# Another order of loads at the start of stick-breaking attention, and other places for two sets of transposes

## The chip, the cores and the metric

The kernel runs on one core of a Trainium2 chip. The metric is the device time of one execution in microseconds (us), the median of several runs. The core has TensorE (matmuls and transposes; PE in the profile, PEld its weight loads), VectorE (DVE), ScalarE (ACT), GpSimd (POOL) and SyncE (SP). In this kernel SP issues most loads and POOL most stores; each works through its queue in order, so an issue that waits holds up all that stand behind it.

## The reference

One step of an encoder layer for a prompt of 1024 tokens and a sample of 32 tokens with a cache of 512, model width 1024, everything in float32. What matters here:

```python
ada = silu(c) @ w_ada + b_ada        # (1024 x 6144): shift1, scale1, gate1, shift2, scale2, gate2
h   = rms_norm(x, g_pre_mix) * (1 + scale1) + shift1
p   = h @ w_in                       # q-latent | kv-latent | rope key | q_b | k_b | v_b | gate A | gate B
z   = einsum('bqhd,bshd->bhqs', q_b, k_b) * 64 ** -0.5      # stick-breaking attention, 8 heads of 64
sp  = where(mask, softplus(z), 0);  later = cumsum(sp, reverse) - sp
o_b = einsum('bhqs,bshd->bqhd', where(mask, exp(log_sigmoid(z) - later), 0), v_b)
```

The new rows of k_b and v_b are outputs too. Latent attention (o_a), two gated projections, an output projection and a gated convolutional feed-forward layer follow; conv_w, conv_b, g_pre_ffn and the latent gains are vectors that these later stages need.

## The kernel before, in words

**Products.** Each float32 operand is held as a high part (rounded to fp32r) and a low part (the rest), and a product takes three fp32r matmuls: high by high, high by low, low by high. Splitting costs one ScalarE instruction for the high part (`hi`, L65) and one VectorE subtraction for the low one (`lo`, L68). A weight tile of 128 columns is loaded by SP into a `wr` buffer of 128 x 1024 (two buffers) and split into `wh` and `wl` (two buffers each); a `wr` buffer is free once its split is done.

**Stages.** `stage_h` makes h, transposed. `stage_qkv` makes the queries, keys and values of the stick-breaking heads. `stage_sb` runs that attention, with the gate columns of w_in and the adaptive weights as fill. `stage_lat`, `stage_mla`, `stage_merge`, `stage_up` and `stage_down` follow.

**`stage_qkv`.** The column tiles are 128 wide; tile p holds heads 2p and 2p + 1. First the query tile 0, the key tile 0 (copied to S0, whose first 1024 columns are also called S1) and one latent tile (`lf`) are made one by one, in three blocks of 352 tokens by `mtile`. The other ten tiles are made in five pairs by `pair`: each pair is computed as seven half-size products on sums and differences of the two weights (`ra`, `rb`) and of h (T1 to T4, made by `sums`). The sums of weights are written to S1 (L575, L576). Each finished tile is handed to `after`: a key tile gets a high part (`KH`, in an `sg` buffer, of which there are two), nine transposes into natural row order that are copied (L462) and stored to the output (L468) in three steps, and at the end its low part, in place; `spill` (L449) stores high and low parts in DRAM scratch (`qh`, `ql`, `kh`, `kl`). Value tiles go to `vd`. The steps of `after` are a generator, put in the list `back`; `bg(n)` advances it by n steps. For the key tile 0 this is `bg(4)`, behind all three blocks of the latent tile and behind the store of it (`l2d`, L645).

**Late vectors.** `late_vectors` (called behind the second pair) loads nine rows of vectors into an `sg` buffer by POOL, transposes them in seven transposes (L159) and copies them out.

**The start of `stage_sb`.** The pools of `stage_qkv` are released and the new ones take their place. On the right side lie, in order of address, T4, T3, T1, T2 (two tiles of 8448 bytes a partition each), ending at h; the new pool `sb` (V1, KL1, Q1, KH1, small tiles, V0, KL0, Q0, KH0, 4096 bytes each) ends at the same edge, so KL0, Q0 and KH0 lie where T2 lay. A new tile waits only for the old tiles under it. `begin(h)` issues six loads for head h of a pair by `queries` (L1074) and one for V (L1096 in the first pair, L1070 afterwards).

**The order.** In `sb_attend` TensorE, ScalarE and VectorE follow the written list ORDER (manual_schedule); `S0.0` is a score block, `T0.0` a block of transposes, `V3.0` a product with values, `f` one step of the fill, the first digit the head and query block (0 to 3 is the first head, 4 to 7 the second), and `then` hangs loads on entries. S1.1 is the fourth score block and takes the `s` bank of S0.0. The fill is the generator of `gates`: for each of 16 gate tiles two adaptive weights (`ada_step`, L204, 512 KB each, matmuls L206), then 24 steps of three matmuls. Everything else, the queues of SP and POOL and the other engines outside such a section, is ordered by the compiler's scheduler, by readiness and the order of the program. `issue_after(x)` makes what is traced inside it come behind x in the queue of x's engine, without waiting for x to finish. `sb_sample`, traced behind the four pairs, begins with a memset of QZ (L953), a tile of the pool `att`, which takes the place of the released left-side pools.

## Time and profile before

| what | us |
|---|---|
| median of three runs | 1723.23 (1721.87 to 1725.38) |
| the profiled execution | 1717.57 |
| its span, first to last instruction | 1715.8 |
| TensorE busy | 1662.9 |
| VectorE busy | 1272.7 |
| ScalarE busy | 992.6 |
| GpSimd busy | 293.7 |

Times in the profile's rows count from the start of the span. A timeline row gives start, duration, engine, line, operation, tiles (out<-in), shapes, how often, and in brackets the idle time of the engine just before and what ended it. `SPq` and DMA rows are issues, not transfers; a row of DMA issues gives the size of each and the median time from issue to landing. A row of a window gives the stretch and its length, busy time and number of instructions of PE, PEld, DVE, ACT and POOL, the granted clock of TensorE, the share of the DMA engines and GB/s. A row of waits gives the total, how often, and the longest.

### The profile page before, as it was taken

The page shows a single profiled execution, that of the slowest core. Times are in us where ns is not written, and L with a number is a line of the kernel's source. Part 1 is how long each engine was busy: PE and PEld are TensorE (multiplying, and loading weights), DVE is VectorE, ACT ScalarE, POOL GpSimd, SP SyncE. Part 2 cuts the span into 40 slices and gives each one's busy share as a digit, 9 for nine tenths or more (in the row PEclk, how much of TensorE's full clock was granted, in tenths as well). Part 3 has the DMA queues.
Part 4 walks back from the last instruction along what each step waited for, and adds up shares of the span by engine and source line. Part 5 has one row for each costly group of instructions (what it writes and reads, how often), then busy time and mean ns, then how long its engine had stood idle before and what let it go on. Part 6 is the DMA issues. An engine that isn't in the chain of part 4 may idle for free. (4 is left out here: it accounts for less than half of the span.)

```text
span 1715.8 us, 30290 instructions
## 1 busy us (share of the span) xinstructions
PE 1662.9 (97%) x11646; PEld 1514.0 (88%) x11646; DVE 1272.7 (74%) x2129; ACT 992.6 (58%) x1934; POOL 293.7 (17%) x564
## 2 busy tenths in 40 slices
PE   6999799999999999999999999999999999999997
PEld 3999799999899899998889789999999999977885
DVE  4854497979794588888776779887787787788456
ACT  4534386979794567777773376544444444544442
POOL 2113311111111131111000121121121122110013
PEclk8999999999999999999999999999999999999999
DMA  9235687555633331222174531423323333697643
GB/s 328 89 116 185 234 229 199 157 166 164 170 117 94 118 94 53 68 61 73 55 276 149 184 123 50 155 93 129 130 99 133 133 101 134 225 346 243 219 138 120
DMA packets 185984, 255.20 MB, mean 149 GB/s; under 512 B 14702, under 2 KB 125568, under 8 KB 185840
## 3 DMA queue, kind: packets, MB, share of 16 engines
q1 hardware_dynamic: 165712, 194.63, 36.3%
q0 software_dynamic: 19904, 58.56, 9.6%
q8 instruction: 91, 1.49, 0.4%
q14 instruction: 53, 0.43, 0.1%
q10 hardware_dynamic: 224, 0.09, 0.0%
HBM read 187.86 MB, written 64.57 MB: 147 GB/s over the span
## 5 line engine op out<-in xcount | busy, mean ns | idle before, releaser
L65 ACT ACTIVATE wh<-wr 128x1024 fp32r<-128x1024 f32 (+5 forms) x163 | 132.2, 820 | 220.3 <-PE s L2010 81.7
L68 DVE TENSOR_TENSOR wl<-wr,wh 128x1024 fp32r<-128x1024 f32 (+5 forms) x163 | 150.0, 929 | 86.4 <-ACT wh L65 86.0
L72 PE MATMUL mm<-hh,wh 128*128 128x352 f32 x456 | 154.0, 338 | 0.0
L73 PE MATMUL mm<-hl,wh 128*128 128x352 f32 x456 | 149.2, 327 | 0.4 <-DVE hl L302 0.3
L74 PE MATMUL mm<-hh,wl 128*128 128x352 f32 x456 | 148.4, 326 | 0.0
L2009 PE MATMUL mm<-T,wh 128*128 128x256 f32 (+1 forms) x376 | 108.5, 289 | 0.0
L2011 PE MATMUL mm<-T,wl 128*128 128x256 f32 (+1 forms) x376 | 107.5, 287 | 0.3 <-DVE wl L68 0.2
L2010 PE MATMUL mm<-T,wh 128*128 128x256 f32 (+1 forms) x376 | 107.3, 286 | 0.0
L2009 PE MATMUL s<-T,wh 128*128 128x256 f32 (+1 forms) x348 | 99.7, 287 | 2.5 <-ACT wh L65 2.5
L2011 PE MATMUL s<-T,wl 128*128 128x256 f32 (+1 forms) x348 | 99.7, 286 | 0.4 <-DVE wl L68 0.4
L2010 PE MATMUL s<-T,wh 128*128 128x256 f32 (+1 forms) x348 | 99.4, 286 | 0.0
L68 DVE TENSOR_TENSOR wl<-S,wh 128x1024 fp32r<-128x1024 f32 (+1 forms) x55 | 59.3, 1079 | 51.0 <-ACT wh L65 50.7
L72 PEld LDWEIGHTS mm<-hh,wh 128*128 128x128 f32 x456 | 86.4, 189 | 7.3 <-ACT o L756 3.3
L73 PEld LDWEIGHTS mm<-hl,wh 128*128 128x128 f32 x456 | 86.4, 190 | 3.2 <-DVE hl L302 1.8
L2150 DVE SCALAR_TENSOR_TENSOR u<-u,c,u 128x1058 f32<-128x1058 f32 x68 | 87.0, 1317 | 2.1 <-ACT u L2147 0.8
L74 PEld LDWEIGHTS mm<-hh,wl 128*128 128x128 f32 x456 | 86.4, 189 | 0.4 <-issue 0.3
L770 PE MATMUL tr<-c,A 128*128 128x128 f32 x576 | 83.8, 274 | 0.8 <-ACT A L729 0.3
L65 ACT ACTIVATE wh<-S 128x1024 fp32r<-128x1024 f32 (+1 forms) x55 | 51.8, 943 | 46.5 <-PE s L2010 13.4
L2009 PE MATMUL tr<-T,wh 128*128 128x272 f32 (+1 forms) x272 | 77.8, 286 | 0.0
L2011 PE MATMUL tr<-T,wl 128*128 128x272 f32 (+1 forms) x272 | 77.7, 286 | 0.0
L2010 PE MATMUL tr<-T,wh 128*128 128x272 f32 (+1 forms) x272 | 77.4, 284 | 0.0
L770 PEld LDWEIGHTS tr<-c,A 128*128 128x128 f32 x576 | 67.3, 141 | 7.7 <-DVE PTl L68 1.4
(754 smaller groups left out, 5793.7 us busy)
## 6 DMA issues: line engine op xcount, KB each, us to landing
wr<-in_w_ada_dram SPq DMA_DIRECT2D x48, 512.0 KB, 6.4
wr<-in_w_up_dram SPq DMA_DIRECT2D x44, 512.0 KB, 3.9
dr<-in_w_down_dram SPq DMA_DIRECT2D x43, 512.0 KB, 6.0
wr<-in_w_in_dram SPq DMA_DIRECT2D x33, 512.0 KB, 4.7
wr<-gdn SPq DMA_DIRECT2D x30, 512.0 KB, 4.3
gdn<-u POOLq DMA_DIRECT2D x23, 512.0 KB, 5.4
gd<-nat POOLq DMA_DIRECT2D x48, 176.0 KB, 3.7
t<-gd SPq DMA_DIRECT2D x16, 528.0 KB, 5.0
```

The lines of the kernel that those rows point to most:

```text
L65: self.nc.scalar.activation(out, in_, AF.Identity, scale=scale)
L68: return self.nc.vector.tensor_tensor(out, full, hi.bitcast(F32), ALU.subtract)
L72: m(ps, lh, rh, start=start, stop=False)
L73: m(ps, lh, rl, start=False, stop=False)
L74: self.pe = m(ps, ll, rh, start=False, stop=stop).ins
L770: self.nc.tensor.transpose(tr[:, (2 * s + q) * P : (2 * s + q + 1) * P], at[q][:, b * P : b * P + P], self.idt)
L2009: m(ps[:, :n], w[0][:, k], x[0][:, k, c], start=first and k == 0, stop=False, skip_group_check=True)
L2010: m(ps[:, :n], w[0][:, k], x[1][:, k, c], start=False, stop=False, skip_group_check=True)
L2011: i = m(ps[:, :n], w[1][:, k], x[0][:, k, c], start=False, stop=k == 3, skip_group_check=True)
L2150: nc.vector.scalar_tensor_tensor(y, u[:, w : w + YW], self.cvT[:, w, cc : cc + 1], y, ALU.mult, ALU.add)
```

## The change

The first key tile's steps are advanced by two behind each block of the latent tile, in place of four behind the last. The late vectors are loaded behind the second pair and transposed behind the third. All adaptive weights of `ada_step` are queued behind the last of the six query and key loads of the first head of the first pair. The second head's loads are issued in every pair at S2.0a (queries and keys) and S2.1a (values); before, this was so for the first pair alone, both at S2.0a, and for the others at S7.1b and V7.0 of the pair before.

```diff
--- before.py
+++ after.py
@@ -159,15 +159,24 @@
         self.nc.tensor.transpose(ps[:, :n], v, self.idt[:n, :n])
         return ps[:, :n]
 
+    def late_loads(self, v):
+
+        a = self.a
+        rows = [(r0, n, 0, a[g][0]) for r0, n, g in ((0, 8, "g_pre_ffn"), (8, 3, "g_q_lat"), (11, 2, "g_kv_lat"))]
+        rows += [(0, 44, w + 1, a["conv_w"][0, w] if w < 3 else a["conv_b"][0] if w == 3 else a["state_ffn_conv"][0, 0, w - 4])
+                 for w in range(6)]
+        for r0, n, w, x in rows:
+            self.nc.gpsimd.dma_start(v[r0 : r0 + n, P * w : P * w + P], x.rearrange("(k p) -> k p", p=P))
+        return v
+
     def late_vectors(self, v):
 
         nc, a = self.nc, self.a
         ps = self.bank("tr")
         dma = nc.gpsimd.dma_start
-        self.rows_T(ps, v[:13, 0:P], ((0, 8, a["g_pre_ffn"][0]), (8, 3, a["g_q_lat"][0]), (11, 2, a["g_kv_lat"][0])), dma)
+        self.rows_T(ps, v[:13, 0:P], (), dma)
         for w in range(6):
-            x = a["conv_w"][0, w] if w < 3 else a["conv_b"][0] if w == 3 else a["state_ffn_conv"][0, 0, w - 4]
-            self.rows_T(ps[:, 44 * (w + 1) :], v[:44, P * (w + 1) : P * (w + 2)], ((0, 44, x),), dma)
+            self.rows_T(ps[:, 44 * (w + 1) :], v[:44, P * (w + 1) : P * (w + 2)], (), dma)
         nc.vector.tensor_copy(self.gvT[:, 8:21], ps[:, :13])
         nc.vector.tensor_copy(self.cvT.rearrange("p w c -> p (w c)"), ps[:, 44 : 44 * 7])
 
@@ -201,7 +210,8 @@
         ps = self.bank("mm")
         for i, (v, k) in enumerate(self.ada_todo[:n]):
             w = self.tl(pool, [P, D], F32, "wr")
-            nc.sync.dma_start(w, a["w_ada"][0, k * P : (k + 1) * P, v * D : (v + 1) * D])
+            with self.tc.issue_after(self.begun):
+                nc.sync.dma_start(w, a["w_ada"][0, k * P : (k + 1) * P, v * D : (v + 1) * D])
             for j in range(4):
                 nc.tensor.matmul(ps[32 * j : 32 * j + 32, :256], self.cT[:, k], w[:, j * 256 : j * 256 + 256],
                                  start=i == 0, stop=i == n - 1)
@@ -642,12 +652,14 @@
         raws = [(raw(col("v", 0)), raw(col("v", 1)))]
         for c0, n, ps in self.mtile(wh, wl, self.Hh, self.Hl, self.BLK, KT, "mm mm pv"):
             nc.scalar.copy(lf[:, c0 : c0 + n], ps[:, :n])
+            bg(2)
         nc.gpsimd.dma_start(self.l2d, lf)
-        bg(4)
         for i, (ta, tb) in enumerate(pairs):
             pair(i, ta, tb, *U[i % 2 * 2 : i % 2 * 2 + 2])
             if i == 1:
-                self.late_vectors(sg().bitcast(F32))
+                late = self.late_loads(sg().bitcast(F32))
+            elif i == 2:
+                self.late_vectors(late)
         self.in_w.append(self.w_in_tile(2208))
         for r, c in self.SB:
             nc.gpsimd.dma_start(self.sbd[r, c], self.sb[r, c])
@@ -1066,7 +1078,8 @@
         t = lambda n: self.tl(S, [P, TP], F32R, n)
 
         def values(p, h):
-            V[h] = t(f"V{h}")
+            if p:
+                V[h] = t(f"V{h}")
             nc.sync.dma_start(V[h].bitcast(F32).rearrange("r (t d) -> r t d", t=8), self.vd[p][:, :, h])
 
         def queries(p, h):
@@ -1079,7 +1092,7 @@
             d(KH[h][o], "kh")
             d(Q[h][o], "ql")
             d(self.KLz[h][r], "kl")
-            d(self.KLz[h][o], "kl")
+            return d(self.KLz[h][o], "kl").ins
 
         def first(h):
             V[h], self.KLz[h], Q[h], KH[h] = t(f"V{h}"), t(f"KL{h}"), t(f"Q{h}"), t(f"KH{h}")
@@ -1091,11 +1104,8 @@
         self.diagonals(S)
         first(0)
 
-        def begin(h):
-            queries(0, h)
-            nc.sync.dma_start(V[h].bitcast(F32).rearrange("r (t d) -> r t d", t=8), self.vd[0][:, :, h])
-
-        begin(0)
+        self.begun = queries(0, 0)
+        values(0, 0)
 
         def score(h, ps, i, c0, n):
             q = slice(i * P, (i + 1) * P)
@@ -1105,10 +1115,9 @@
         fill = self.gates()
         E = mybir.EngineType
         for p in range(4):
-            then = {} if p == 3 else {"S3.1b": lambda: queries(p + 1, 0), "V3.0": lambda: values(p + 1, 0),
-                                      "S7.1b": lambda: queries(p + 1, 1), "V7.0": lambda: values(p + 1, 1)}
-            if p == 0:
-                then["S2.0a"] = lambda: begin(1)
+            then = {"S2.0a": lambda: queries(p, 1), "S2.1a": lambda: values(p, 1)}
+            if p < 3:
+                then.update({"S3.1b": lambda: queries(p + 1, 0), "V3.0": lambda: values(p + 1, 0)})
             with self.tc.manual_schedule(engines={E.PE, E.Activation, E.DVE}):
                 self.sb_attend(score, lambda b, h: V[h][:, b * P : b * P + P], self.store(self.obd[p]), fill, then)
         self.in_w.append(self.next_w.pop(0))
```

## The prediction

> **What bounds the kernel now.** I read the page first: its first line says which engine to count on.

> ```profile
> PE 1662.9 (97%) x11646; PEld 1514.0 (88%) x11646; DVE 1272.7 (74%) x2129; ACT 992.6 (58%) x1934; POOL 293.7 (17%) x564
> ```

> TensorE works 1662.9 of 1715.8 us, so only its 53 us of idle time, and time at a reduced clock, can be won. The view of waits, TensorE alone, says what the idle time is for; these three rows lead to places that the diff touches.

> ```profile
> PE s L1102 <- DMA Q<-ql: 9.3, 1, 9.3
> ...
> PE s L2009 <- ACT wh L65: 2.5, 1, 2.5
> ...
> PE mm L206 <- DMA wr<-in_w_ada_dram: 2.0, 2, 1.2
> ```

> The largest is the start of the stick-breaking stage. The timelines of TensorE and of SP's queue show it from both sides.

> ```profile
> 187.26 0.29 PE L2011 MATMUL mm<-T,wl 128*128 128x272 f32 x1
> ...
> 210.08 0.58 PE L1102 MATMUL s<-KH,Q 128*128 128x256 f32 x1 [9.27 <-DMA Q<-ql]
> 212.56 0.55 PE L1103 MATMUL s<-KL,Q 128*128 128x256 f32 x1 [1.91 <-DMA KL<-kl]
> ...
> 214.11 1.94 PE L206 MATMUL mm<-wr,cT 128*32 128x256 f32 x16
> ...
> 218.59 0.39 PE L1102 MATMUL s<-KH,Q 128*128 128x512 f32 x1
> ```

> ```profile
> 186.10 0.34 SPq L204 DMA_DIRECT2D wr<-in_w_ada_dram  x1
> ...
> 199.56 0.34 SPq L204 DMA_DIRECT2D wr<-in_w_ada_dram  x1
> 200.00 0.51 SPq L1074 DMA_DIRECT2D Q<-qh  x1
> ...
> 202.49 1.68 SPq L1074 DMA_DIRECT2D KL<-kl  x2
> ...
> 215.26 0.40 SPq L82 DMA_DIRECT2D wr<-in_w_in_dram  x1
> ```

> ```profile
> SPq L204 <- DVE wl L68: 19.8, 3, 12.3
> ```

> The second adaptive weight needs a `wr` buffer, which the split of the gate weight frees (VectorE `wl`); SP stands 12.3 us behind it and then issues the first head's loads. They could have gone earlier: their tiles KL0, Q0, KH0 end at the edge of the released pool where T2 lay, and T2's last product is the row at 187.26.

> The second stall lies in the first pair of column tiles: 0.38 + 2.52 + 0.39 = 3.3 us on TensorE.

> ```profile
> 88.61 0.44 PE L456 MATMUL tr<-c,fq 128*128 128x128 f32 x2 [0.38 <-DVE fq L566]
> 91.58 0.39 PE L2009 MATMUL s<-T,wh 128*128 128x256 f32 x1 [2.52 <-ACT wh L65]
> ...
> 92.72 0.39 PE L2011 MATMUL s<-T,wl 128*128 128x256 f32 x1 [0.39 <-DVE wl L68]
> ```

> ```profile
> 82.18 1.22 DVE L68 TENSOR_TENSOR S<-S,sg 128x1024 fp32r<-128x1024 f32 x1
> ...
> 90.17 0.69 DVE L575 TENSOR_TENSOR S<-wr 128x512 f32<-128x512 f32 x1
> ```

> ```profile
> 82.85 0.53 POOL L645 DMA_DIRECT2D l2d<-q  x1 [8.38 <-ACT q L644]
> ...
> 85.44 0.58 POOL L449 DMA_DIRECT2D kl<-S  x1
> ```

> ```profile
> kl<-S POOLq DMA_DIRECT2D x1, 512.0 KB, 4.6
> ```

> L575 makes the sums of weights in S1, the buffer in which the first key row still stands. Its low half leaves it through `kl`, issued at 85.44, landed 4.6 us later: 90.1, and L575 starts at 90.17. So this stall is the first key row's.

> **The change, part by part.**

> *First key row.* Moved: nine transposes, three copies, one VectorE subtraction (1.22 us at 82.18), the three output DMAs and `kl`; nothing is added. They now stand behind the first and second column block of the latent row, not behind the third. Before, most of the transposes ran here:

> ```profile
> 81.28 0.82 PE L456 MATMUL tr<-c,S 128*128 128x128 f32 x6
> ```

> TensorE does not idle in this stretch, so moving them costs nothing there. The subtraction no longer waits for those six, and POOL no longer has `kl` behind `l2d`, which waits for the third block (82.85). By my estimate the subtraction ends 4 us or more sooner, `kl` lands at 86 or before instead of 90.1, and L575 with the split after it (1.4 us on from L575 to TensorE at 91.58) is done before 88. Saved: 3.3 us of stall. The clock comes on top, read from the windows.

> ```profile
> 93.40:96.80 3.40, 3.40 (x18) 3.40 (x17) 2.28 (x4) 0.53 (x1) 0.00 (x0) 0.50 0.56 172
> 98.00:132.00 34.00, 34.00 (x284) 33.95 (x283) 17.91 (x33) 13.04 (x28) 5.39 (x10) 1.00 0.34 105
> 210.00:216.20 6.20, 4.22 (x23) 2.25 (x24) 0.12 (x1) 1.67 (x6) 0.00 (x0) 0.50 1.05 395
> ```

> At a granted 0.50, 18 matmuls took 3.40 us; at 1.00, 284 took 34.00 us, 0.12 each, so 18 are worth 2.16: 1.2 us more. Together **-4.5 us** (bounds: 0, if `kl` keeps its place; -4.5). [...]

> *Late vectors.* The loads stay; seven transposes and two copies come one pair later, more than 20 us behind loads that kept TensorE waiting by 1.07. The `sg` buffer is held one pair longer; the key rows of the next pair can take the other one.

> ```profile
> 140.61 0.26 PE L159 MATMUL tr<-c,sg 44*128 44x44 f32 x1 [1.07 <-DMA sg<-in_conv_w_dram]
> ```

> **-1.1 us** (0 to -1.1).

> *First head's loads.* Six issues of 0.5 to 0.6 us move ahead of both adaptive weights. In the queue they now wait for T2's last product, 187.6, and are out by 192; at the longest landing of such a load anywhere in 180 to 330 us, the last row below, they are there at 201, when TensorE comes (210.08 - 9.27 = 200.8).

> ```profile
> DMA to landing us min/median/max: 3.4/6.2/9.1
> ```

> The added order delays the first adaptive weight by about 6 us (186.1 to 192), needed no earlier than 202; the second still goes at 199.56. Behind the tied loads stand, besides the two weights, the bias loads and the next gate weight, which wait for those weights' matmuls anyway. So 11.2 us of waiting go. What is late next? The second adaptive weight lands at 203.5 to 204.5 (3.9 us below, up to 5) and TensorE is there at 202.2: 1 to 2 us. Then it has five steps of gate matmuls, 2.6 us, and at about 207 it needs S1.1, whose bank is free only when VectorE has worked through S0.0. VectorE is not free:

> ```profile
> 216.08 0.27 DVE L953 MEMSET QZ<- 128x256 f32 x1 [10.58 <-PE mm L206]
> ```

> ```profile
> 204.94 1.05 POOL L449 DMA_DIRECT2D ql<-fq  x2 [0.66 <-DVE fq L488]
> ```

> ```profile
> DMA packets 2434, 5.75 MB, mean 338 GB/s; under 512 B 279, under 2 KB 1143, under 8 KB 2433
> ...
> ql<-fq POOLq DMA_DIRECT2D x2, 512.0 KB, 10.0
> ```

> The memset has nothing to do with the matmul that its row names; QZ lies where the released pools lay, and their last readers are the two `ql` spills, issued at 204.94 and 205.5 and landed 10 us later, at 215 to 216. The memset is first in VectorE's queue, and S1.1 (218.59) follows their landing by 2.7 us. This was hidden behind the loads and comes to light now. The spills land earlier, since the DMA queues are lighter: of the 5.75 MB that move in 199 to 216 us, six loads of 256 KB and V (512 KB), 2.1 MB, are gone, and one 512 KB gate weight comes in from 215.26 once its buffer frees at 203. Net 1.6 MB at the full 400 GB/s of the window at 210 (395) is 3.9 us: they land at 212, S1.1 starts at 214.7 instead of 218.6. But TensorE has then idled for 7 us and restarts at half clock with full work: one such stretch cost 1.2 us above; I take 1.5. **-2.4 us.** Bounds: the spills land no earlier (+1.5), or 3.2 us after issue as `kl` below, 208.7 (-5.7); without the memset in the way -9 (the rival below).

> ```profile
> kl<-fq POOLq DMA_DIRECT2D x1, 512.0 KB, 3.2
> ```

> *Second head's loads.* Per pair the same seven issues, moved from the end of the pair before to this pair's first third; in the first pair only V moves, by one step. Nothing waits in SP's queue for them, as their tiles' last readers are long done. TensorE's two waits for adaptive weights (2.0 us, 1.2 of it in the first) come behind a second head's V in SP's queue; the first of them:

> ```profile
> 288.90 0.56 SPq L1070 DMA_DIRECT2D V<-vd  x1
> 290.02 0.35 SPq L204 DMA_DIRECT2D wr<-in_w_ada_dram  x1
> ```

> With V away the weights can land sooner, by 2.0 us in all at most, and some of it comes back at the new place, where the same seven loads share the queues with other weights. I take **-0.8 us** (-2.0 to +1; what is worse is rival C).

> Sum: -4.5 - 1.1 - 2.4 - 0.8 = **-8.8 us**. The profiled execution took 1717.57 us (span 1715.8 and 1.8 around it), 5.7 below the median of the three runs, 1723.23. Its own time would become 1708.8; on the median the forecast is **1714.4 us**.

> **The rivals.**

> *A, the memset is not in the way.* If the compiler's order puts QZ behind S0.0's work, S1.1 waits only for ScalarE, some 9 us sooner than now. The part is worth -9, the sum -15.4: 1707.8. Against it: nothing in the diff touches sb_sample, and VectorE still idles at that place.

> *B, the first key row changes nothing.* The compiler orders these engines itself; if `kl` still comes behind `l2d`, 90.1 stays. Sum -4.3: 1718.9. For it: VectorE has other sums to make before 82; against it: among them are T4's (L555, L556), which the fourth product alone needs, and the row's steps now stand ahead of them in the program.

> *C, slower: the second head's loads meet the adaptive weights.* Their new place, 298 to 311 us in the second pair, is just ahead of this one:

> ```profile
> 308.48 0.33 SPq L204 DMA_DIRECT2D wr<-in_w_ada_dram  x1
> ```

> ```profile
> wr<-in_w_ada_dram SPq DMA_DIRECT2D x1, 512.0 KB, 3.9
> ```

> ```profile
> 313.22 0.42 PE L206 MATMUL mm<-wr,cT 128*32 128x256 f32 x4
> ```

> ```profile
> wr<-in_w_ada_dram SPq DMA_DIRECT2D x1, 512.0 KB, 10.2
> ```

> It lands in 3.9 us and TensorE comes after 4.74. In the first pair, with the second head's loads around it, the one issued at 221.46 took 10.2. The same in three pairs costs 3 x (10.2 - 4.7) = 16.5 us: 1730.9. It decides once the landing passes 4.7 us. Against it: the loads have 5 us and more to clear.

> *D, the loads do not come early,* because the compiler puts another waiting transfer ahead of them. Then the start stays and the adaptive weights come later still: -6.4 + 0 to 2, 1718.

> **How the numbers follow.** The range runs from 1706.6 to 1722.8. Forecast 0.45, A 0.15, B 0.20, C 0.12, D 0.08. A measurement of this kernel tells about 0.2%, 3.4 us, from no change, so faster means below 1719.8: the forecast, A, half of B (0.10) and 0.05 of D make 0.75; the rest of B and D makes 0.13 for the same; C is 0.12 for slower. The range takes in A with the second head at its best, 1707.8 - 1.2 = 1706.6, and B with the start at its worst bound, 1718.9 + 3.9 = 1722.8; C is left out.

> **What would show it.** Right: L1102's loads issued near 188 and no wait of L1102 on a DMA; TensorE then stops at S1.1, and VectorE's QZ memset ends its wait at the landing of `ql`, near 206 (all times 5.6 earlier); no wait at 88 to 93 and no half clock behind it; no wait at L159. Wrong: `kl` still behind `l2d` (B); waits of L206 that grow in the later pairs (C); the six loads behind an adaptive weight (D); a new wait in the column pairs from the held `sg` buffer, which would make the first two terms too large.

## The result, and the profile after

| | before | after |
|---|---|---|
| median of seven runs, us | 1723.23 (1718.79 to 1726.65) | 1714.69 (1712.39 to 1719.77) |
| profiled execution, us | 1717.57 | 1714.10 |
| its span, us | 1715.8 | 1712.3 |

The ratio of the runs is 0.9956, with a 95% interval of 0.9938 to 0.9974: 7.6 us less (4.5 to 10.7). Here and below a gain in us is worked out from the ratio and the median of before. The difference of the two medians can be another: 8.5 us here, and up to 2.4 us more or less than the ratio's in the runs below. The two profiled executions differ by 3.5 us only, because the one of before was among the shortest of its kernel.

Most lines of the changed kernel have moved: L206 is now L216, L204 L214, L449 L459, L575 L585, L582 L592, L953 L965, L1074 L1087, L1102 L1112, L2009 to L2011 L2018 to L2020. TensorE's waits of after, those of the touched places:

```profile
PE s L1112 <- DVE A L739: 5.4, 2, 4.6
PE mm L216 <- DMA wr<-in_w_ada_dram: 4.6, 3, 2.7
...
PE mm L216 <- ACT T L65: 1.8, 1, 1.8
```

The 11.2 us for Q and KL and the wait at L159 are gone. In their place stand the s bank (L1112), two adaptive weights (the row that names ACT T is the first of them; the weight landed 0.1 us before that, and in a second execution of this kernel, e_after, the same wait is put down to it) and, in the first pair, a copy on ScalarE (below) instead of the split of the weight sums. The page of the profile gives TensorE 1663.3 us of busy time, 1662.9 before: the 3.5 us between these two executions are idle time.

**First pair.** GpSimd's, TensorE's and ScalarE's timelines of after, and the landing of `kl`:

```profile
79.08 0.55 POOL L459 DMA_DIRECT2D kl<-S  x1
```

```profile
kl<-S POOLq DMA_DIRECT2D x1, 512.0 KB, 4.5
```

```profile
86.41 0.29 PE L2020 MATMUL s<-hh,wl 128*128 128x272 f32 x1
89.28 0.39 PE L2018 MATMUL mm<-T,wh 128*128 128x256 f32 x1 [2.58 <-ACT q L592]
```

```profile
86.17 0.63 ACT L65 ACTIVATE wh<-S 128x512 fp32r<-128x512 f32 x1 [8.62 <-DVE S L586]
...
87.05 0.63 ACT L65 ACTIVATE wh<-S 128x512 fp32r<-128x512 f32 x1
87.89 1.08 ACT L65 ACTIVATE T<-fq 128x1056 fp32r<-128x1056 f32 x1 [0.21 <-DVE fq L566]
88.88 0.64 ACT L592 COPY q<-mm 128x256 f32<-128x256 f32 x2
```

`kl` is issued 6.4 us sooner and has landed at 83.6; L585 starts at 83.62. Of the 6.4, 1.6 are not the change's: this execution had 6.8 us of half clock before 40 us where that of before had 10.2, so all its times at 78 us lie 1.6 us ahead. Yet TensorE still waits 2.58 us, for the X bank. Its products ended at 83.8, but their copy to Q1 (L592) stands in ScalarE's queue behind the split of the sums (L65 at 86.17 and 87.05), which waits for S1, and behind T4's split (87.89). VectorE works on T4's sums (L565) between those of the weights:

```profile
83.62 0.69 DVE L585 TENSOR_TENSOR S<-wr 128x512 f32<-128x512 f32 x1 [6.60 <-issue]
84.23 1.25 DVE L565 TENSOR_TENSOR fq<-hh,fq 128x1056 f32<-128x1056 f32 x1
```

**Late vectors.** Before, the seven transposes stood one by one between products; after, they stand in one row. First before, then after:

```profile
141.15 0.29 PE L2011 MATMUL mm<-T,wl 128*128 128x272 f32 x1
141.36 0.26 PE L159 MATMUL tr<-c,sg 44*128 44x44 f32 x1
141.55 0.39 PE L2009 MATMUL mm<-T,wh 128*128 128x272 f32 x1
```

```profile
149.46 0.72 PE L159 MATMUL tr<-c,sg 13*128 13x13 f32 x7
```

**Start of the stage.** SP's queue, TensorE, VectorE and ScalarE of after:

```profile
182.04 0.52 SPq L1087 DMA_DIRECT2D Q<-qh  x1
...
185.95 0.58 SPq L1083 DMA_DIRECT2D V<-vd  x1
186.63 7.74 SPq L214 DMA_DIRECT2D wr<-in_w_ada_dram  x2
```

```profile
195.02 0.36 PE L1112 MATMUL s<-KH,Q 128*128 128x256 f32 x1
...
201.21 1.08 PE L216 MATMUL mm<-wr,cT 128*32 128x256 f32 x8 [2.67 <-DMA wr<-in_w_ada_dram]
...
211.56 0.76 PE L1112 MATMUL s<-KH,Q 128*128 128x512 f32 x1 [4.61 <-DVE A L739]
```

```profile
209.28 0.27 DVE L965 MEMSET QZ<- 128x256 f32 x1 [9.32 <-DMA ql<-fq]
```

```profile
210.28 0.49 ACT L721 ACTIVATE A<-s 128x384 f32<-128x384 f32 x1 [4.69 <-DMA sbd<-sb]
```

S0.0 starts with no wait. S1.1 waits for VectorE, whose memset of QZ ends its wait 0.2 us behind the landing of the second `ql` spill (issued at 199.9 and landed at 209.1). The windows show what it costs beside the waits: 0.50 twice.

```profile
199.95:206.75 6.80, 5.54 (x23) 4.51 (x23) 0.00 (x1) 1.67 (x6) 1.91 (x5) 0.50 1.05 408
...
210.20:217.00 6.80, 5.44 (x19) 5.24 (x20) 5.61 (x11) 5.14 (x13) 0.00 (x0) 0.50 1.06 214
```

**Second head.** SP's queue near the end of the first pair, first in before and then in after, and TensorE behind it in after:

```profile
274.82 1.23 SPq L1074 DMA_DIRECT2D KL<-kl  x2
...
277.04 0.53 SPq L204 DMA_DIRECT2D wr<-in_w_ada_dram  x1
```

```profile
272.40 0.52 SPq L214 DMA_DIRECT2D wr<-in_w_ada_dram  x1
272.97 0.45 SPq L1087 DMA_DIRECT2D Q<-ql  x1
273.47 0.88 SPq L1087 DMA_DIRECT2D KL<-kl  x1
...
283.58 0.45 SPq L1087 DMA_DIRECT2D KL<-kl  x1
284.12 0.56 SPq L1083 DMA_DIRECT2D V<-vd  x1
285.29 0.35 SPq L214 DMA_DIRECT2D wr<-in_w_ada_dram  x1
```

```profile
290.90 0.64 PE L216 MATMUL mm<-wr,cT 128*32 128x256 f32 x8 [1.72 <-DMA wr<-in_w_ada_dram]
```

The loads are still issued in the pair before, most of them within a few us of where they were. The low half of Q and the first half of KL have slipped behind one adaptive weight. The last half of KL has slipped further, from ahead of the bias loads (274.82 to 276.1 before) to just ahead of V and the next adaptive weight. That weight, with 256 KB more ahead of it, lands 5.6 us after its issue instead of 5.0, and TensorE's wait grows from 1.16 to 1.72 us. That the 256 KB are the cause is not shown: e_pad below has the same order of issues, and its wait at this place is 1.08 us.

### The profile page after: what moved, and what is told of

It is laid out like the page before. It is cut to its first block, busy times and chain, and to the rows that moved or that the text cites. A ratio compares the mean times of both kernels' runs of the same rounds, so it can differ in the third digit from the quotient of the medians.

```text
span 1712.3 us, 30291 instructions
## 1 busy us (share of the span) xinstructions
PE 1663.3 (97%) x11646; PEld 1517.1 (89%) x11646; DVE 1274.1 (74%) x2129; ACT 991.4 (58%) x1934; POOL 297.3 (17%) x564
## 5 line engine op out<-in xcount | busy, mean ns | idle before, releaser
L65 ACT ACTIVATE wh<-wr 128x1024 fp32r<-128x1024 f32 (+5 forms) x163 | 132.1, 820 | 224.9 <-PE s L2019 78.6
L68 DVE TENSOR_TENSOR wl<-wr,wh 128x1024 fp32r<-128x1024 f32 (+5 forms) x163 | 151.3, 936 | 84.8 <-ACT wh L65 84.7
L2018 PE MATMUL mm<-T,wh 128*128 128x256 f32 (+1 forms) x376 | 108.7, 289 | 2.6 <-ACT q L592 2.6
L2020 PE MATMUL mm<-T,wl 128*128 128x256 f32 (+1 forms) x376 | 107.6, 287 | 0.3 <-DVE wl L68 0.2
L2018 PE MATMUL s<-T,wh 128*128 128x256 f32 (+1 forms) x348 | 99.4, 286 | 0.0
L2020 PE MATMUL s<-T,wl 128*128 128x256 f32 (+1 forms) x348 | 99.2, 285 | 0.0
L68 DVE TENSOR_TENSOR wl<-S,wh 128x1024 fp32r<-128x1024 f32 (+1 forms) x55 | 59.2, 1078 | 47.4 <-ACT wh L65 47.1
L65 ACT ACTIVATE wh<-S 128x1024 fp32r<-128x1024 f32 (+1 forms) x55 | 51.8, 943 | 55.1 <-PE s L2019 13.4
L2018 PE MATMUL tr<-T,wh 128*128 128x272 f32 (+1 forms) x272 | 77.7, 286 | 0.0
L2020 PE MATMUL tr<-T,wl 128*128 128x272 f32 (+1 forms) x272 | 77.6, 285 | 0.1
L2018 PEld LDWEIGHTS mm<-T,wh 128*128 128x128 f32 x376 | 71.2, 189 | 4.1 <-ACT q L592 2.8
## 6 DMA issues: line engine op xcount, KB each, us to landing
wr<-in_w_ada_dram SPq DMA_DIRECT2D x48, 512.0 KB, 5.8
wr<-in_w_up_dram SPq DMA_DIRECT2D x44, 512.0 KB, 4.0
dr<-in_w_down_dram SPq DMA_DIRECT2D x43, 512.0 KB, 5.9
wr<-in_w_in_dram SPq DMA_DIRECT2D x33, 512.0 KB, 4.8
wr<-gdn SPq DMA_DIRECT2D x30, 512.0 KB, 4.9
gdn<-u POOLq DMA_DIRECT2D x23, 512.0 KB, 5.3
```

The costliest lines, as they stand in the source:

```text
L65: self.nc.scalar.activation(out, in_, AF.Identity, scale=scale)
L68: return self.nc.vector.tensor_tensor(out, full, hi.bitcast(F32), ALU.subtract)
L2018: m(ps[:, :n], w[0][:, k], x[0][:, k, c], start=first and k == 0, stop=False, skip_group_check=True)
L2020: i = m(ps[:, :n], w[1][:, k], x[0][:, k, c], start=False, stop=k == 3, skip_group_check=True)
```

## The experiments

Every kernel was timed against the kernel before, in five rounds. There were four sets, on four chips, and the median of before was between 1718.7 and 1722.9 us by set; so ratios can be compared across sets, and medians within one. Besides the medians I compared the traces by stretches: TensorE's 11646 instructions are counted in order, and a stretch is the time between the starts of the same two of them. Each holds one part of the change. In the profiled execution of before they run from 87.0 to 98.6 us (**key**), 137.3 to 159.7 (**late**), 199.5 to 236.8 (**start**) and 293.3 to 449.7 (**second head**). A stretch is free of what happens elsewhere in that execution; a median is not. Of runs that contain a part, and of runs that lack it, the change of each stretch against the profiled execution of before, in us:

| stretch | runs without the part | runs with it | difference of means |
|---|---|---|---|
| key | 0, 0.2, 0.2, 0.4 | -2.7 (four), -1.2 (two), -1.1 | -2.2 |
| late | 0, 0.6, 3.4, 3.4 | -3.0 (all nine) | -4.8 |
| start | 0, 1.1, 1.1, 2.3 | -0.6, -0.2, 0.0, 0.3, 0.9 | -1.1 |
| second head | 0, 0.2, 0.2, 0.6, 1.4 | 0.7, 1.5, 1.8, 2.4, 3.1, 3.2, 3.3, 3.5, 3.8 | +2.1 |

Runs that alter a stretch in another way are left out of its row. From the scatter of so few executions, the standard errors of the four differences are 0.3, 0.9, 0.5 and 0.4 us. The differences add up to -6.0 us, inside the interval of the runs but short of their -7.6. In the two executions profiled first the four stretches nearly cancel (+0.2 us). Their difference of 3.5 us lies in places that the change doesn't touch, 1.5 of it before 46 us and 0.8 at the end, so a single pair of profiles can't price the parts.

### Each part alone

The main lines of the four edits:

```diff
 (p_key: before, and)
             nc.scalar.copy(lf[:, c0 : c0 + n], ps[:, :n])
+            bg(2)
         nc.gpsimd.dma_start(self.l2d, lf)
-        bg(4)
 (p_late: before, with late_loads behind pair 1 and late_vectors behind pair 2)
 (p_tie: before, and)
+            with self.tc.issue_after(self.begun):
+                nc.sync.dma_start(w, a["w_ada"][0, k * P : (k + 1) * P, v * D : (v + 1) * D])
 (p_head2: before, and)
+            then = {"S2.0a": lambda: queries(p, 1), "S2.1a": lambda: values(p, 1)}
+            if p < 3:
+                then.update({"S3.1b": lambda: queries(p + 1, 0), "V3.0": lambda: values(p + 1, 0)})
```

> The kernel before, with only the first key row's steps moved (two of them behind each of the first two column blocks). Theory of the prediction, its first term alone: -4.5 us, and no wait of TensorE in 86 to 93 us. Rival, from the trace of after: kl lands 6 to 7 us sooner and L575 follows it, but the X bank's copy to Q1 in ScalarE's queue ends TensorE's wait instead, one wait of 2 to 3 us stays near 89 us and half a clock behind it: 0 to -1.5 us.

Median 1721.11 against 1722.90, ratio 0.9988 (0.9976 to 1.0001): -2.1 us (-4.1 to +0.2). The rival's wait is there, as in after:

```profile
90.90 0.39 PE L2009 MATMUL mm<-T,wh 128*128 128x256 f32 x1 [2.58 <-ACT q L582]
```

In this execution no reduced clock follows it, and the stretch gains 2.7 us; where one follows, as in after, 1.1 to 1.2. So the half clock is worth 1.5 us here, where the prediction took 1.2. It followed in all four executions without the part and in three of the seven with it; whether the part makes it rarer, or this was chance, so few can't show.

> The kernel before, with only the late vectors' transposes one pair later. Theory of the prediction, its second term alone: -1.1 us, the one wait at L159. Rival, from the trace of after: -3 us, because the seven transposes now stand in one row instead of one by one between products, each of which cost some 0.3 us more there.

Median 1716.30 against 1722.90, ratio 0.9958 (0.9944 to 0.9973): -7.2 us (-9.6 to -4.7), more than either theory gave. The stretch is -3.0 against the profiled execution of before, as the rival has it. But in two of the four executions that have the old order (p_key and p_head2) half a clock follows the wait at L159, which costs another 3.4 us; the profile of before had been spared. In p_key:

```profile
141.40:148.20 6.80, 6.80 (x29) 6.11 (x30) 1.39 (x3) 0.87 (x3) 1.30 (x2) 0.50 0.40 145
```

So the part is worth 3.0 or 6.4 us, by execution, and 4.8 as the difference of means, at the near edge of the interval. What the rest of the 7.2 is, no trace shows.

> The kernel before, with only the first head's six loads tied ahead of the adaptive weights, V of the first head right behind them. Theory of the prediction, its third term alone: -2.4 us. Rival, from the trace of after: the 11.2 us of waits for loads go, and waits for both adaptive weights (1 to 3 us each), for S1.1 (4 to 5 us) and half a clock for 10 us and more take their place: -1.5 to +1.5 us.

Median 1722.69 against 1722.90, ratio 0.9998 (0.9985 to 1.0012): -0.3 us (-2.6 to +2.1). Waits of 1.7 and 2.8 us for the adaptive weights and 4.3 us at S1.1 took the place of those for the loads: the rival. The interval holds the theory's -2.4 too; it is the waits that decide.

> The kernel before, with only the second head's loads recorded in their own pair. Theory of the prediction, its fourth term alone: -0.8 us, loads issued in the first third of each pair. Rival, from the trace of after: the compiler issues them early, at the end of the pair before, within 5 us of where they were: 0, between -1 and +1 us.

Median 1724.88 against 1722.90, ratio 1.0005 (0.9993 to 1.0018): +0.9 us (-1.2 to +3.1). The loads hardly move, as the rival says; but its 0 is too kind. The two waits for adaptive weights are 1.9 and 2.3 us (1.2 and 0.8 before) with half a clock behind each. The stretch, which ends ahead of the second wait, is 3.2 us longer; between its end and 521 us of before, with that wait in it, another 2.8 are lost. Over all runs the stretch is 0.7 to 3.8 with the part and 0 to 1.4 without: it costs some 2 us, which the medians alone don't resolve.

### The changed kernel again, and what the row of transposes is worth

> The changed kernel again, beside the three runs that follow. The four parts alone gave ratios of 0.9988, 0.9958, 0.9998 and 1.0005; if they add up and do not touch one another: 0.9949, -8.7 us. If the late vectors alone are the whole gain: 0.9958, -7.2 us.

Median 1714.04 against 1721.62, ratio 0.9951 (0.9933 to 0.9970): -8.4 us. The four parts' results add up to -8.7; the late vectors alone, -7.2, lie in the interval too, so the times don't tell the two apart.

```diff
             i = m(ps[:, :n], w[1][:, k], x[0][:, k, c], start=False, stop=k == 3, skip_group_check=True)
+            if self.single:
+                with self.tc.issue_after(i.ins):
+                    next(self.single, None)      # one of the seven transposes
```

> The changed kernel, with the seven late transposes one by one behind every third product of the next pair, their data landed long before. If standing alone between products is what costs (some 0.35 us each before): 2 to 2.8 us longer than the changed kernel, with no wait at L159. If only the waits for the loads cost before: the same as the changed kernel within 0.5 us in the profile.

Ratio 0.9966 (0.9950 to 0.9982): -5.9 us, 2.6 less gain than e_after, with intervals that overlap. The late stretch settles it: -1.2 instead of -3.0, so 1.8 us, with no wait; 2 to 2.8 had been expected. TensorE's timeline:

```profile
148.84 0.28 PE L2025 MATMUL mm<-hh,wl 128*128 128x256 f32 x1
149.06 0.26 PE L159 MATMUL tr<-c,sg 44*128 44x44 f32 x1
...
149.58 0.28 PE L2025 MATMUL mm<-hh,wl 128*128 128x256 f32 x1
```

The row at 149.58 is the third product behind the transpose. From L2025 to the next L2025 pass 0.74 us; three products alone take 0.36. A single transpose thus costs 0.38 us, seven of them 2.6; in one row the seven cost about 0.75 (the row at 149.46 in after). The old wait of 1.1 us and this 1.8 make 2.9 of the 3.0 of the stretch.

### The first pair's queues

```diff
+            if i == 0:
+                for b in range(2):
+                    x1 = nc.scalar.copy(Q1[:, cs[b]], X[b][:, : ns[b]]).ins
+                with self.tc.issue_after(x1):
+                    w1, w2 = half(s1a), half(s1b)
+                low = self.low               # the last lo of w2
...
+            if i == 0:
+                with self.tc.issue_after(low):
+                    next(S)                  # T4
```

> The changed kernel, with the X bank's copies to Q1 ahead of the split of the first sums in ScalarE's queue, and T4's sums behind that split in VectorE's queue, in the first pair only. If these two are all that took the place of the old stall: no wait of TensorE over 0.5 us at 85 to 92 us and no half clock behind it, 2.6 us of stall and 1 to 1.7 us of clock, -3.5 to -4.3 us against the changed kernel. If T4's hi and lo come too late for the fourth product, a new wait of 1 to 2 us near 98 us takes part of it: -1 to -2.5 us. If the late landing of kl still decides: no change.

Ratio 0.9933 (0.9916 to 0.9950): -11.5 us, 3.1 more than e_after. ScalarE, TensorE and the window behind:

```profile
85.35 0.39 ACT L589 COPY q<-mm 128x272 f32<-128x272 f32 x1 [1.12 <-PE mm L2032]
86.59 1.16 ACT L65 ACTIVATE wh<-S 128x512 fp32r<-128x512 f32 x2 [0.86 <-DVE S L586]
```

```profile
87.94 0.29 PE L2032 MATMUL s<-hh,wl 128*128 128x272 f32 x1
88.06 0.28 PE L2030 MATMUL mm<-T,wh 128*128 128x256 f32 x1
```

```profile
90.80:94.10 3.30, 3.30 (x29) 3.30 (x28) 3.30 (x4) 0.39 (x1) 0.00 (x0) 1.00 1.02 263
```

No stall and no reduced clock. The key stretch is 5.5 us shorter than before, and 0.7 come back by 104 us, 0.5 of it in a new wait for a copy on ScalarE (97.47 us): -4.8. That is about the forecast's -4.5, had with two more moves that the change doesn't make.

### The start

```diff
         QZ = self.tl(self.sm2, [P, 4, 64], F32, "QZ")
-        nc.vector.memset(QZ, 0.0)
+        with self.tc.issue_after(self.dv):   # the last L739 traced
+            nc.vector.memset(QZ, 0.0)
```

> The changed kernel, with the QZ memset behind the first stage's VectorE work instead of ahead of it. Theory of the prediction: the memset, which waits for both ql spills, is what holds S1.1; without it S1.1 starts some 3.5 us sooner and its wait of 4.6 us falls to 1 us or less. Rival: the wait moves to a1.0, whose A buffer is free only when the sbd spill has landed at 210.2, and TensorE stops 2 to 3 us later in its program for about as long: -0.5 to -1.5 us in all.

Ratio 0.9949 (0.9932 to 0.9967), -8.8 us, no more than e_after within its interval. TensorE:

```profile
206.06 0.47 PE L1113 MATMUL s<-KH,Q 128*128 128x512 f32 x1 [1.16 <-DVE A L739]
...
210.17 0.90 PE L782 MATMUL tr<-c,A 128*128 128x128 f32 x3 [3.11 <-ACT A L741]
```

and ScalarE ahead of it:

```profile
208.01 0.49 ACT L721 ACTIVATE A<-s 128x384 f32<-128x384 f32 x1 [3.92 <-DMA sbd<-sb]
```

Both theories hold, one behind the other: the memset did hold S1.1, and without it the wait moves to T0.0, because a1.0's buffer is free only when the `sbd` spill has landed. The stretch is -0.3.

```diff
-                spill("ql", p, low)          # e_start: for p = 2, 3 behind both sbd spills
...
-        values(0, 0)                         # e_start: at E0.0, behind the second adaptive weight
```

> The changed kernel with three things at the start of the stick-breaking stage: the QZ memset late, the two sbd spills ahead of the last two ql spills, and V of the first head behind the second adaptive weight instead of ahead of the first. If the bytes ahead of them in the DMA queues set when the weights and the sbd spill land: 0.5 MB less is 1.3 us at 400 GB/s, so the waits for the two weights fall from 1.4 to 1.6 and 2.7 us to about 0.3 and 1.4, T0.0's wait from 3.1 (with the memset late) to about 1, -3 to -4 us against the changed kernel. If the landing does not follow the order in the queues: -0.5 us or less, as the memset alone gave.

Ratio 0.9939 (0.9922 to 0.9957), -10.5 us. The start stretch is -3.5, against 0.1 as the mean of the five runs with the part as it is. The first adaptive weight, no longer behind V, landed 8.7 us after its issue (11.1 in after), and its wait is gone. What waits are left (the first row's 4.4 us are the second weight's 2.0 and the 2.4 near 290 us):

```profile
PE mm L216 <- DMA wr<-in_w_ada_dram: 4.4, 2, 2.4
...
PE s L1123 <- DVE A L746: 3.0, 2, 2.5
...
PE tr L789 <- ACT A L748: 1.2, 2, 0.8
```

The second weight's wait fell from 2.7 to 2.0 us (1.4 expected), T0.0's from 3.1 in e_qz to 0.8 (1 expected). Both agree with the first theory, that the bytes ahead in the queues set the landing; one run with three moves can't show more. The share of each move was not measured, and the first weight came 2.4 us sooner behind its issue, where 0.5 MB at 400 GB/s (408 in after's window at 199.95) would make 1.3. But S1.1 waits 2.5 us again (1.16 in e_qz, 4.1 in e_all), because a third buffer comes next. ScalarE, ahead of it:

```profile
205.16 0.38 ACT L728 ACTIVATE A<-s 128x256 f32<-128x256 f32 x1 [2.66 <-DMA vd<-sg]
```

The second score block can't be worked on until a `vd` store has landed, and in ScalarE's queue the rest of S0.0's work stands behind it. This wait is there in after too (2.79 us), hidden behind the memset.

> The same, with the first pair's queues as in the run of the changed kernel with the X bank's copies first, which gave -3 us. Both together if they do not touch one another: -6 to -7 us against the changed kernel, a ratio of 0.991 to before; -3.5 if the start gives nothing.

Ratio 0.9923 (0.9907 to 0.9939), -13.2 us; median 1706.74. The key stretch is again -5.5, the start -3.5: both gains stand beside each other.

```diff
+            then = {} if p == 3 else {"S3.1b": lambda: queries(p + 1, 0), "V3.0": lambda: values(p + 1, 0),
+                                      "S7.1b": lambda: queries(p + 1, 1), "V7.0": lambda: values(p + 1, 1)}
```

> The same again, with the second head's loads of pairs 1 to 3 recorded at the end of the pair before, as in the kernel before. If their own pair costs through the longer wait for an adaptive weight near 290 us (1.7 to 2.3 against 1.2 us) and the half clock behind it: 1 to 2.5 us less than with them in their own pair. If the compiler issues them at nearly the same time either way: the same within 0.5 us in the profile.

Ratio 0.9912 (0.9895 to 0.9930), -15.1 us; median 1706.04, the fastest here, and it beats both kernels. Against e_all the medians differ by less than their intervals; the stretch of the second head is 0.2 instead of 2.4 in the profiled executions, with a wait of 1.45 us at that place and no reduced clock behind it.

### Work in the wait

```diff
+            if x == "S1.1" and self.pad:
+                self.pad, tr = False, self.bank("tr")
+                for _ in range(32):
+                    nc.tensor.transpose(tr[:, :P], self.idt, self.idt)
```

> The changed kernel, with 32 transposes of the identity into a spare bank put on TensorE just ahead of the first S1.1, inside its wait of 4.6 to 5.5 us; they add work whose results nothing reads. 32 at 0.13 us are 4.2 us. If the reduced clock follows from how little TensorE did in the 3.4 us before: S1.1 starts no later, the clock stays at 1.00 in 208 to 215 us, and the stage gets back some 2 us. If the clock drops anyway for another reason, the 32 run at half speed, 8.4 us, and S1.1 starts some 3 us later: +2 to +4 us.

TensorE, and the window, first of e_pad and then of e_after at the same place:

```profile
206.54 3.65 PE L705 MATMUL tr<-c 128*128 128x128 f32 x32
211.24 0.47 PE L1116 MATMUL s<-KH,Q 128*128 128x512 f32 x1 [1.05 <-DVE A L743]
```

```profile
206.20:215.30 9.10, 8.05 (x61) 7.65 (x61) 5.86 (x14) 5.37 (x14) 0.14 (x1) 1.00 1.06 263
```

```profile
208.50:215.30 6.80, 4.57 (x16) 4.36 (x17) 5.51 (x13) 4.82 (x11) 0.00 (x0) 0.50 1.05 216
```

With 32 transposes in the wait, alone on TensorE for 3.65 us, the clock stayed at 1.00 in 206.20 to 215.30, and the start stretch is 2.0 us shorter than the mean of the five, though S1.1 starts no sooner (210.73 in e_after): as the first theory has it. It is one execution; in all five with this start as it is, half clock set in during the wait at S1.1 or right behind it. The ratio, 0.9954 (0.9938 to 0.9970), does not show this gain; 2 us are within its interval.

## Why the prediction was right or wrong, point by point

The forecast was -8.8 us, measured were -7.6 (4.5 to 10.7) and -8.4. The sum is right by luck: no term has its size, and the errors cancel.

**First key row (-4.5, worth about -2).** `kl` landed at 83.6, sooner than the forecast's 86, and L585 followed it; rival B fell. What failed is the step from there, "the split after it is done before 88. Saved: 3.3 us of stall". The step looked only at what the stalled matmul had waited for. The next in line, the X bank's copy, stood in the same ScalarE queue behind that split, with T4's in between; and T4's sums on VectorE kept the weight sums from being split sooner. e_key2 shows it: with those two moved the stretch gives 4.8.

**Late vectors (-1.1, worth -3.0, and -6.4 where the clock had dropped).** The direction is right, the size too small by two things. The transposes' cost was counted as the one visible wait; that they were scattered between products, 0.38 us each, stood in the timeline and was not priced (e_scatter: 1.8). And the clock's cost was read from the one profiled execution of before, which had none behind this wait.

**First head's loads (-2.4, worth about -1).** Each mechanism came as forecast: issue by T2's release, no wait at S0.0, a stall for the second weight, the QZ memset ending with `ql`. The sizes failed: the first adaptive weight, "needed no earlier than 202", was needed 1.8 us before it came, since V and six loads stood ahead of it; the second's wait is 2.7 instead of 1 to 2; and `ql` landed at 209.1, where the forecast's 212 means 206.5 (the stage before ended 5.5 us earlier here). Its step "2.1 MB, are gone, and one 512 KB gate weight comes in" counted too little: V and the first adaptive weight had moved as well, into 186 to 198 (issue rows above; they took 9.5 and 11.1 us to land), so what they delayed could land later. e_start fits that; the share of each was not measured. Half clock came twice, not once for 1.5. Rival A fell, since the memset is in the way. Its price of 9 us fell with it: e_qz takes the memset out of the way and gains 0.3, because the buffers held by the `sbd` and `vd` stores come next. Rival D fell, as the six loads went out at 182.

**Second head's loads (-0.8, worth about +2).** The failed step is "moved from the end of the pair before to this pair's first third". They were not moved by more than some places in the queue; the compiled order had the last word. The wait behind them, 1.2 to 1.6 us in the five executions without the part and 1.1 to 2.4 in the nine with it, now costs the clock in six of those nine. Why it grows is not shown. Rival C had the right place for a loss, an adaptive weight behind these loads, but not the mechanism: behind the first pair's start no adaptive weight took more than 6.8 us to land.

The signs named at the end of the prediction came out so: issue near 182 (188 less 5.5) right; S1.1 behind the memset right, its time wrong; no wait at 88 to 93 wrong; no wait at L159 right; L216's waits that grow, listed as a sign of C, came.

## What to carry to other kernels

When a stall is to go, follow the queue of the engine that released it one step further: what the stalled instruction needs next may stand in that same queue, and moving it is half the gain. A load moved in the program has moved only if the compiled queue says so. Price a stall with the clock behind it from several executions, not one, and small transposes by whether they stand alone (0.38 us each here) or in a row (0.75 for seven).

## What the runs showed of the hardware

**The clock.** Of eleven executions with the first pair's stall of 2.5 to 2.9 us, half a clock followed in seven: in after, for one, but not in p_key, with 2.58 us in each. Of fourteen with the wait near 290 us, it followed in none of the seven waits up to 1.66 us and in six of the seven from 1.72 to 2.42. The stretches of reduced clock lasted one to four times 3.4 us (3.4 us from 93.36 and 10.2 from 206.00 in before).

```profile
84.86:88.27 3.41, 1.90 (x16) 1.67 (x14) 3.41 (x5) 1.87 (x4) 0.57 (x1) 1.00 0.00 0
...
87.31:90.72 3.41, 1.44 (x12) 1.44 (x13) 3.41 (x5) 2.00 (x4) 0.57 (x1) 1.00 0.40 159
```

TensorE idled 1.5 us in the one and 2.0 in the other: an edge between two intervals cut the first stall in two, and no half clock followed it. The ends of matmuls are modelled, so the 1.9 us are approximate.

**Transposes between products.** A float32 transpose of 44 rows alone between fp32r products cost 0.38 us (e_scatter); seven in a row cost 0.75 together (after).
